# Dilated projections and all gates by seven half-size products, with the sums of h's quarters made in the memory branch

## The chip, the cores and the metric

The kernel runs on one core of one Trainium2 chip. The metric is the device time in microseconds from the first to the last instruction of one launch. The kernel before takes 2093.71 us (median of three runs, 2093.24 to 2095.69). One more execution was profiled: it took 2091.8 us, and the span of its trace is 2090.0 us. All durations below come from that execution.

## The reference

One decoder layer on 1024 tokens of width 1024, in float32. Cut to what matters here:

```python
h = rms_norm(x, g_pre_mix)
proj = h @ w_in                       # columns: MLA latents, dilated q/k/v, memory q, gates
y_mla = mla(...)                      # 8 heads, low-rank q and kv
y_dil = dilated_mixture(proj[..., OFF_KR:OFF_DIL])   # 3 groups x 4 heads x 128, q, k and v: 36 blocks of 128 columns
y_mem = mem_attention(...)            # 4 heads against 256 memory tokens
gates = sigmoid(proj[..., OFF_MEMQ:] + b_gate)       # 3 x 1024 columns: 24 blocks of 128
merged = sum(gates[n] * (y[n] @ w_br[n]) for n in 3 branches)
x = x + rms_norm(merged @ w_o)
x = x + rms_norm(conv_ffn(rms_norm(x)))              # up 1024 -> 2 x 2816, conv, silu gate, down
```

A dilated head regroups the tokens by their residue (dilation 1, 4 or 16) and attends within a band of 128 keys before each query. Its three groups are combined by their softmax denominators.

## The kernel before

Everything is kept with features on the partitions and tokens along the free axis. Each float32 operand of a product is split in two float32r parts, hi and lo (`split`: ACT writes hi at L141, DVE or POOL writes lo = x - hi at L146), and every product is three matmuls, hi*hi, lo*hi and hi*lo (`mm3`: L156, L157, L158). A projection of 128 columns over 1024 tokens is thus 8 blocks of k, times 3, times two halves of 512 tokens: 48 matmuls of 512 columns.

A second form, `winograd`, takes two blocks of 128 columns at once. It cuts the weights in four quarters (two column blocks, two halves of k) and h in four (two halves of k, two halves of the tokens), and makes the eight half-size products from seven. Sums of the weights are made on POOL (L1183, L1184, L1189, L1196), each of the seven sums is split, the products (L1179) go into four PSUM banks `f`, and DVE, ACT and POOL combine them (L1186 to L1201). A pair of blocks takes 7 x 4 x 3 = 84 matmuls of 512 columns. The right-hand sides are quarters of h and four sums of quarters, T1 to T4, which `winograd_rhs` makes (POOL and DVE at L1107 and the lines after it).

The stages, in the order of the program: startup (norm, h split into `ht`), the memory branch (to about 143 us), the latents of MLA (to about 200), MLA's eight heads (to 419.7), the dilated branch (to 926), the rest of the gates, then merge, out projection and the two FFN stages. Six of the eight tiles of h are stored to DRAM at the start (`spill_h`), because MLA uses their room for k, q and v, and loaded again at its end (`reload_h`). The dilated branch makes q, k and v of two heads at a time by plain projections, group 0's values with the tokens on the partitions (`values_by_token`, matmuls of 256 columns), and keeps them split as pages. `dil_head` then walks four pairs of 128 queries: scores, softmax (L803 to L811), transposes, the product with v, eviction (L843, L844). The first gate blocks are made by plain projections (`early_gates` and `gate_direct`), the other ten pairs by `winograd` in `all_gates`, with the outputs of the dilated and MLA branches (`dil_out`, `mla_out`) between.

Buffers are slots of named pools (`wr` raw weights, `wh` and `wl` split weights, `pg` pages, `p`, `pt`, `ht`), all of one tile pool that lives as long as the kernel. A list scheduler with a timing simulation of its own decides the order of every engine's instructions, SP's loads and stores (`load`, L161) among them. What stands in SP's queue is issued strictly in that order: an issue that waits for a buffer holds up all that stand behind it.

Of the kernel before, what the change touches and what calls it, by code (L numbers as in the profile page):

```python
# [20 lines left out]
P = 128  # L21
# [66 lines left out]
NPG, NWR, NWH, NP, NPT = 13, 4, 4, 3, 4  # L88
# [4 lines left out]
SPILLED = ((0, 0), (1, 0), (0, 1), (1, 1), (0, 2), (0, 3))  # L93


class Kern:
    def __init__(self, tc, ctx, ins, out):
        self.tc, self.nc, self.out = tc, tc.nc, out
        self.i = ins
        self.sb = ctx.enter_context(tc.tile_pool(name="sb", bufs=1))  # L100
        self.dr = ctx.enter_context(tc.tile_pool(name="dr", bufs=1, space=DRAM))
        self.n = 0
# [6 lines left out]
    def t(self, tag, bufs, shape, dt=F32):  # L109
        return self.sb.tile(shape, dt, tag=tag, bufs=bufs, name=self.name(tag))  # L110
# [10 lines left out]
    def arena(self, dt=F32R):  # L121
        return self.t("ht", 8, [P, 2, 1024], dt)
# [175 lines left out]
    def feature_unit(self, w, m0, rhs, k=KD, m=P):  # L298

        for half in range(2):  # L300
            u = self.ps("u")
            for kk in range(k):
                self.mm3(u[:m], w(kk, m0, m), [r(kk)[:, 512 * half:512 * half + 512] for r in rhs],
                         kk == 0, kk == k - 1)
            yield half, u


    def new_h(self):
        self.hA = [[self.arena() for _ in range(4)] for _ in range(2)]
        self.set_h()  # L310

    def set_h(self):
        self.hT = [lambda k, a=a: a[k // 2][:, k % 2, :] for a in self.hA]

    def startup(self):
# [39 lines left out]
        def blocks(b0):  # L355
            for q in range(4):
# [5 lines left out]
                sl = slice(b0 * P, (b0 + 2) * P)  # L362
                self.split(self.hA[0][q][:, :, sl], self.hA[1][q][:, :, sl], tp)
# [27 lines left out]
    def spill_h(self):  # L391

        self.hD = self.dr.tile([6, P, 2, S], F32, name="hD")
        for n, (hl, q) in enumerate(SPILLED):
            self.nc.gpsimd.dma_start(self.hD[n], self.hA[hl][q].bitcast(F32))

    def reload_h(self):
        for n, (hl, q) in enumerate(SPILLED):
            t = self.arena()
            for j in range(2):  # L400
                self.load(t[:, j, :].bitcast(F32), self.hD[n][:, j, :])
            self.hA[hl][q] = t
        self.set_h()
# [52 lines left out]
    def latents(self):  # L456
# [59 lines left out]
        for half in range(2):  # L516
            sl = slice(512 * half, 512 * half + 512)
            u = self.ps("u")
            for k in range(KD):
                for hl in range(2):  # L520
                    nc.tensor.matmul(u, wkr[:, k, :], self.hT[hl](k)[:, sl], start=k == hl == 0,
# [6 lines left out]
        self.cq = [lambda k, hl=hl: self.cT[hl][k] for hl in range(2)]  # L528
        self.ckv = [lambda k, hl=hl: self.cT[hl][3 + k] for hl in range(2)]
# [20 lines left out]
    def mla_start(self):  # L550
# [3 lines left out]
        self.kA, self.qA, self.vA = [[self.arena() for _ in range(2)] for _ in range(3)]  # L554
# [10 lines left out]
    def mla(self):  # L565
# [13 lines left out]
        self.w_first = self.w_cols(self.i["w_in"], OFF_DIL, page=True)  # L579
# [12 lines left out]
    def mla_v(self, hf):  # L592
# [8 lines left out]
        for b2 in range(8 // n):  # L601
            u = self.ps("u", (P, n, 256))
            for a in range(n):
                b = n * b2 + a
                for k in range(2):
                    self.mm3(u[:, a, :], [self.ckv[hl](k)[:, b * P:(b + 1) * P] for hl in range(2)],
# [91 lines left out]
    def dilated(self):  # L698
        nc, i = self.nc, self.i
# [3 lines left out]
        for hp in range(2):  # L703
            for g in range(3):
                col = lambda part: OFF_DIL + ((part * 3 + g) * DIL_HG + 2 * hp) * DH
                qk = []
                for part in range(2):
                    w = self.w_first if hp == g == part == 0 else self.w_cols(i["w_in"], col(part))
                    pair = []
                    if hp == g == part == 0:  # L710
                        first = [(half, self.ps(("u", "s")[j])) for j in range(2) for half in range(2)]
                        for kk in range(KD):
                            for x, (half, u) in enumerate(first):
                                self.mm3(u, w(kk, x // 2 * P, P), [r(kk)[:, 512 * half:512 * half + 512] for r in self.hT],
                                         kk == 0, kk == KD - 1)
                    for j in range(2):
                        d = [self.pg(dt=F32R) for _ in range(2)]
                        dil = PERM[g]
                        sc = DH ** -0.5 if part == 0 else 1.0
                        for half, u in first[2 * j:2 * j + 2] if hp == g == part == 0 else self.feature_unit(w, j * P, self.hT):  # L720
                            hs = slice(512 * half, 512 * half + 512)
                            if g == 0:
                                self.split(d[0][:, hs], d[1][:, hs], u, sc)
                                continue
                            n = 512 // dil
                            uv = u.rearrange("p (l r) -> p l r", r=dil)
                            ls = slice(half * n, (half + 1) * n)
                            if part == 0:
                                dv = [self.perm(t, g)[:, ls, :] for t in d]
                                self.split(dv[0], dv[1], uv, sc)  # L730
                                continue
# [702 lines left out]
```

## Time and profile before

| | |
|---|---|
| time, median of three runs | 2093.71 us |
| profiled execution, its span | 2091.8 us, 2090.0 us |
| PE busy | 1970.1 us, 94% |
| DVE, ACT, POOL busy | 1375.8 (66%), 927.0 (44%), 637.4 us (30%) |
| mean granted TensorE clock | 0.985 |
| dilated branch | 419.7 to about 926 us |
| gates, merge | to about 1160, to 1293 us |
| DMA traffic | 217.81 MB, mean 104 GB/s |

Times in the rows are microseconds from the start of the span. Matmuls are pipelined: a group's mean (394 ns for 512 columns) is a latency, and what one costs the engine is the distance from its start to the next one's. L followed by a number is a line of the kernel. SPq is SP's sequencer, which issues DMAs. The granted clock (PEclk) is a share of the higher of TensorE's two levels.

### The profile page before, as it was taken

What the parts mean: (1) busy time and instruction counts of PE and PEld (TensorE: products, weight loads), DVE (VectorE), ACT (ScalarE), POOL (GpSimd) and SP (SyncE); (2) the same over time, 40 slices, a digit from 0 to 9 for tenths busy, and PEclk for the clock granted to TensorE, in tenths of its full rate; (3) what the DMA queues carried; (4) which work ended last, traced back from release to release, by engine and by line L of the source; (5) the groups of instructions that cost most, each with busy time, mean ns of one, the idle gap of its engine ahead of it and who ended that gap; (6) DMA issues with size and microseconds to landing.
All of it is one profiled execution on the core that took longest, in us unless ns stands there. A gap on an engine that the chain in (4) does not pass through costs nothing.

```text
span 2090.0 us, 25550 instructions
## 1 busy us (share of the span) xinstructions
PE 1970.1 (94%) x9550; PEld 1639.2 (78%) x9550; DVE 1375.8 (66%) x1944; ACT 927.0 (44%) x1737; POOL 637.4 (30%) x417
## 2 busy tenths in 40 slices
PE   6999889799999999998899999998999999989994
PEld 6887677689888988876787888887888888768863
DVE  7645777725354354478655566658777777699999
ACT  6544565624354244444334332334454445455433
POOL 3100111100010000025454040004555555487766
PEclk9999999999999999999999999999999999999997
DMA  8411101341322221212665762231222222433322
GB/s 278 163 64 36 26 22 41 116 132 43 89 72 60 82 82 46 57 47 87 201 216 198 267 225 102 101 91 60 91 73 88 83 91 71 149 133 101 121 81 81
DMA packets 150858, 217.81 MB, mean 104 GB/s; under 512 B 22737, under 2 KB 114558, under 8 KB 149966
## 3 DMA queue, kind: packets, MB, share of 16 engines
q1 hardware_dynamic: 137422, 192.93, 28.8%
q0 software_dynamic: 13312, 23.25, 3.2%
q8 instruction: 75, 1.23, 0.2%
q14 instruction: 49, 0.40, 0.1%
HBM read 159.13 MB, written 55.85 MB: 103 GB/s over the span
## 4 chain that ended last, share of the span: by engine, by line
PE 59%; issue 17%; DVE 14%; DMA 4%; ACT 3%; POOL 2%; SPq 0%; DVEq 0%; POOLq 0%; ACTq 0%
PE f L1179 20%; PE u L156 7%; PE u L157 6%; PE u L158 6%; PE f L156 4%; PE f L157 4%; PE f L158 4%; PE f L1258 3%; DVE wl L146 3%; DVE wh L146 3%; DVE pt L146 2%; DVE ht L1263 2%; PE o L827 1%; POOL oD L689 1%; DMA wr<-dD 1%
## 5 line engine op out<-in xcount | busy, mean ns | idle before, releaser
L156 PE MATMUL u<-ht,wh 128*128 128x512 f32 x672 | 264.4, 394 | 0.9 <-ACT p L467 0.4
L157 PE MATMUL u<-ht,wh 128*128 128x512 f32 x672 | 264.2, 393 | 0.0
L158 PE MATMUL u<-ht,wl 128*128 128x512 f32 x672 | 263.3, 392 | 0.0
L141 ACT ACTIVATE wh<-wr 128x512 fp32r<-128x512 f32 (+3 forms) x164 | 127.3, 798 | 152.9 <-PE u L157 47.2
L1179 PE MATMUL f<-ht,wh 128*128 128x512 f32 x636 | 159.3, 394 | 8.9 <-ACT wh L141 5.7
L1179 PE MATMUL f<-ht,wl 128*128 128x512 f32 x636 | 156.9, 391 | 0.4 <-DVE p L1192 0.4
L1179 PEld LDWEIGHTS f<-ht,wh 128*128 128x128 f32 x636 | 120.6, 190 | 35.8 <-ACT wh L141 6.4
L156 PEld LDWEIGHTS u<-ht,wh 128*128 128x128 f32 x672 | 126.3, 188 | 26.0 <-ACT ht L141 0.9
L158 PEld LDWEIGHTS u<-ht,wl 128*128 128x128 f32 x672 | 126.4, 188 | 25.0
L157 PEld LDWEIGHTS u<-ht,wh 128*128 128x128 f32 x672 | 126.4, 188 | 23.7
L1179 PEld LDWEIGHTS f<-ht,wl 128*128 128x128 f32 x636 | 120.1, 189 | 26.1 <-issue 0.8
L146 DVE TENSOR_TENSOR wl<-wr,wh 128x1024 fp32r<-128x1024 f32 (+2 forms) x74 | 90.9, 1231 | 69.4 <-ACT wh L141 69.2
L846 POOL DMA_DIRECT2D dD<-y x24 | 13.2, 550 | 394.4 <-DVE y L844 394.4
L1179 PE MATMUL f<-pg,wh 128*128 128x512 f32 x444 | 121.0, 394 | 8.7 <-ACT pg L141 5.4
L1179 PE MATMUL f<-pg,wl 128*128 128x512 f32 x448 | 122.4, 393 | 2.9 <-DVE p L1193 1.7
L141 ACT ACTIVATE pg<-u 128x512 fp32r<-128x512 f32 (+2 forms) x90 | 61.2, 680 | 135.1 <-PE u L158 121.4
L1179 PEld LDWEIGHTS f<-pg,wh 128*128 128x128 f32 x444 | 84.3, 190 | 27.7 <-ACT pg L141 6.1
L146 DVE TENSOR_TENSOR pt<-t,pt 128x512 fp32r<-128x512 f32 (+2 forms) x148 | 88.6, 608 | 25.4 <-ACT pt L141 24.4
L1179 PEld LDWEIGHTS f<-pg,wl 128*128 128x128 f32 x448 | 84.6, 189 | 21.3 <-DVE p L1193 2.2
L146 DVE TENSOR_TENSOR pg<-u,pg 128x256 fp32r<-128x256 f32 (+2 forms) x60 | 37.1, 618 | 96.7 <-ACT pg L141 96.5
L141 ACT ACTIVATE pt<-t 128x512 fp32r<-128x512 f32 (+2 forms) x148 | 76.7, 537 | 39.4 <-PE t L671 21.1
L1258 PE MATMUL f<-wh,pt 128*128 128x512 f32 x312 | 80.9, 397 | 13.2 <-DVE wh L146 6.8
(379 smaller groups left out, 5102.4 us busy)
## 6 DMA issues: line engine op xcount, KB each, us to landing
wr<-in_w_in_dram SPq DMA_DIRECT2D x67, 512.0 KB
wr<-in_w_ffn_up_dram SPq DMA_DIRECT2D x88, 256.0 KB
p<-gD SPq DMA_DIRECT2D x24, 512.0 KB
gD<-p SPq DMA_DIRECT2D x22, 512.0 KB
actD<-p SPq DMA_DIRECT2D x22, 512.0 KB
pg<-actD SPq DMA_DIRECT2D x22, 512.0 KB
hD<-ht POOLq DMA_DIRECT2D x6, 1024.0 KB, 7.2
ht<-hD SPq DMA_DIRECT2D x12, 512.0 KB
```

The source lines that it names most:

```text
L141: self.nc.scalar.activation(out, src, AF.Copy, scale=float(scale))
L146: (eng or self.nc.vector).tensor_tensor(out, src, h, op=OP.subtract)
L156: mm(out, l[0], r[0], start=start, stop=False)
L157: mm(out, l[0], r[1], start=False, stop=False)
L158: mm(out, l[1], r[0], start=False, stop=stop)
L689: nc.gpsimd.dma_start(self.oD[:, 64 * h:64 * h + 64, 256 * m:256 * m + 256], y.rearrange("p a q -> p (a q)"))
L827: mm = lambda out, l, r, st: nc.tensor.matmul(out, l, r, start=st, stop=False, skip_group_check=True)
L846: nc.gpsimd.dma_start(self.dD[g, h][:, 512 * (pr // 2):512 * (pr // 2) + 512], y)
L1179: nc.tensor.matmul(out, l[a], r[c], start=start and k == n == 0, stop=k == 3 and n == 2, skip_group_check=True)
L1258: nc.tensor.matmul(u[t], l[j][:, x, t * P:(t + 1) * P], r[j][:, y], start=j == m == 0, stop=j == n - 1 and m == 2, skip_group_check=True)
L1263: vt(acc[d][:, t], acc[d][:, t], u[t], op=OP.add)
```

## The change

All 36 projections of the dilated branch are made by `winograd`, 18 pairs of blocks in the order in which the heads need them, and so are the first two pairs of gate blocks: `early_gates` and `gate_direct` go. q, k and v are kept unsplit, in five pages `rp`, and `dil_head` splits what a pair of queries needs; values always come by transposes. h is stored as quarter tiles (`hQ`, 4 blocks of k by 512 tokens). T1 to T4 are made by the new `spill_T` behind the memory branch and stored to DRAM as 8 tiles of 1 MB (as sixteen stores of 512 KB); only four tiles of h are stored. `reload_h` loads these twelve tiles, 12 MB in place of 6. The pools are opened and closed by stage (`room`), the dilated branch has four `f` banks and one `s` bank in place of two `u` and two `s`, and its first weights are no longer loaded into pages during MLA (`w_first` goes). `mla_out` moves from the dilated branch into the gates.

```diff
     def spill_h(self):
-        self.hD = self.dr.tile([6, P, 2, S], F32, name="hD")
-        for n, (hl, q) in enumerate(SPILLED):
-            self.nc.gpsimd.dma_start(self.hD[n], self.hA[hl][q].bitcast(F32))
+        self.hD = self.dr.tile([4, P, 4, 512], F32, name="hD")
+        for x in range(2):
+            for hl in range(2):
+                self.nc.gpsimd.dma_start(self.hD[2 * x + hl], self.hQ[x, 0][hl].bitcast(F32))
+    def spill_T(self):
+        self.tTD = self.dr.tile([8, P, 4, 512], F32, name="tTD")
+        B = {q: [[t[:, 2 * j:2 * j + 2, :] for j in range(2)] for t in self.hQ[q]] for q in self.hQ}
+        T = self.winograd_rhs(B, lambda n: [[self.pg((P, 2, 512), F32R) for _ in range(2)] for _ in range(2)], True, True)
     def reload_h(self):
+        T = {}
+        for n in (1, 3, 2, 4):
+            T[n] = [self.arena(shape=(P, 4, 512), tag="hT") for _ in range(2)]
+            for hl in range(2):
+                self.load(T[n][hl].bitcast(F32), self.tTD[2 * (n - 1) + hl])
+        for x in range(2):
+            self.hQ[x, 0] = [self.arena(shape=(P, 4, 512)) for _ in range(2)]
...
-        self.w_first = self.w_cols(self.i["w_in"], OFF_DIL, page=True)
...
     def dilated(self):
+        heads = [(g, 2 * hp + j) for hp in range(2) for g in range(3) for j in range(2)]
+        todo = [(part, g, h) for g, h in heads for part in range(3)]
+        done, n = [], 0
+        for i, (g, h) in enumerate(heads):
+            while len(done) < 3 * i + 3:
+                two = todo[len(done):len(done) + 2]
+                cols = [OFF_DIL + ((part * 3 + g1) * DIL_HG + h1) * DH for part, g1, h1 in two]
+                pages = [self.t("rp", NRP, [P, 1024]) for _ in two]
+                self.winograd(self.in_weights(cols), self.B, self.t("S", 1, [P, 2, 4, P]),
+                              self.t("tt", 1, [P, 2, 512]), *pages, [PERM[g1] for _, g1, _ in two])
+                done += pages
+            self.dil_head(g, h, *done[3 * i:3 * i + 3])
...
+            qp = self.t("qs", 2, [P, 2, 256], F32R)
+            self.split(qp[:, 0], qp[:, 1], q[:, 256 * pr:256 * pr + 256], DH ** -0.5)
...
+            self.split(kp[:, 0, :n], kp[:, 1, :n], k[:, k0:k0 + n], eng=nc.gpsimd)
...
     def all_gates(self):
-        self.gate_direct(2, 2, False)
-        turns = [(2, 4), (2, 6)] + [(n, c) for n in range(2) for c in range(0, 8, 2)]
+        turns = [(n, c) for n in (2, 0, 1) for c in range(0, 8, 2)]
...
+            if p % 2 == 0 and 0 < p <= 8:
+                self.mla_out(p // 2 - 1)
...
     def run(self):
+        with self.room("ht"):
+            with self.room("pg", "wh", "wl"), self.room("hx", "p", "pt", "wr"):
...
+                    self.mem_branch()
+                    self.spill_T()
+                    self.latents()
...
+            with self.room("hT"):
+                with self.room("wr", "wv", "S", "tt", "rp", "p2", "e", "ks", "qs", "vs"), \
+                        self.phase(f=4, s=1, t=2, o=1) as self.psum:
+                    self.reload_h()
+                    self.dilated()
+                with self.room("wr", "wv", "S", "tt", "gp", "o4"), self.phase(f=8) as self.psum:
+                    self.all_gates()
```

The scheduler places the instructions anew. Three places on SP follow, each as it stands before and after. The first is the loads of the latents' weights (`wr` from `in_w_in_dram`), at the end of the memory branch. Before:

```order
L161 DMA pg_626<-in_positions_dram 128x1x128
L161 DMA wr_1444<-in_w_in_dram 128x4x256
L161 DMA wr_1450<-in_w_in_dram 128x4x256
L161 DMA wr_1570<-in_w_in_dram 128x8x128
L161 DMA wr_1691<-in_w_in_dram 128x4x256
L291 DMA tD<-pg_625 8x16x128 x2
L161 DMA wr_1697<-in_w_in_dram 128x4x256
```

After:

```order
L1043 DMA tTD<-pg_1451 128x1024
L1043 DMA tTD<-pg_1453 128x1024
L1043 DMA tTD<-pg_1455 128x1024
L1043 DMA tTD<-pg_1459 128x1024
L1043 DMA tTD<-pg_1457 128x1024
L161 DMA wr_1522<-in_w_in_dram 128x4x256
L1043 DMA tTD<-pg_1461 128x1024
L161 DMA wr_1528<-in_w_in_dram 128x4x256
```

Five stores of T (`tTD`, from the pages that the split writes) now stand ahead of the first weights, and more between the rest.

The second is the end of MLA, on SP: the reload of h (`hD` into `ht`), and the first weights of the dilated branch. Before, with the first weights in pages (`pg_4018`, `pg_4024`):

```order
L161 DMA wr_2638<-in_w_ukv_dram 128x2x512
L161 DMA ht_4035<-hD 128x1024 x2
L161 DMA pg_4018<-in_w_in_dram 128x4x256
L161 DMA pg_4024<-in_w_in_dram 128x4x256
L161 DMA ht_4038<-hD 128x1024 x2
L161 DMA ht_4041<-hD 128x1024 x2
L161 DMA ht_4044<-hD 128x1024 x2
L161 DMA ht_4047<-hD 128x1024 x2
L161 DMA wr_4170<-in_w_in_dram 128x4x256
L161 DMA wr_4176<-in_w_in_dram 128x4x256
L161 DMA wr_4294<-in_w_in_dram 128x4x256
```

After, from the second tile of h on (`hT` are the tiles of T1 to T4):

```order
L161 DMA ht_4126<-hD 128x1024 x2
L161 DMA ht_4131<-hD 128x1024 x2
L161 DMA hT_4109<-tTD 128x2048
L161 DMA hT_4110<-tTD 128x2048
L161 DMA hT_4113<-tTD 128x2048
L161 DMA hT_4114<-tTD 128x2048
L161 DMA hT_4117<-tTD 128x2048
L161 DMA hT_4118<-tTD 128x2048
L161 DMA hT_4121<-tTD 128x2048
L161 DMA hT_4122<-tTD 128x2048
L161 DMA ht_4132<-hD 128x1024 x2
L161 DMA wr_4144<-in_w_in_dram 128x4x128 x2
```

The first weights of the dilated branch (`wr_4144`) moved behind eight tiles of T and the last two loads of h.

The third is the end of the gates, on SP: stores of gates (`gD` from the pages of the gates), and the first loads of merge (`yD`, and the weights `in_w_br_mem_dram`). Before:

```order
L161 DMA wr_9762<-yD 128x1024
L985 DMA gD<-p_9352 128x1024
L161 DMA wr_9768<-yD 128x1024
L161 DMA wr_9774<-yD 128x1024
L161 DMA wr_9780<-yD 128x1024
L985 DMA gD<-p_9502 128x1024
L985 DMA gD<-p_9503 128x1024
L161 DMA wr_9786<-in_w_br_mem_dram 128x4x256
L161 DMA wr_9854<-in_w_br_mem_dram 128x4x256
L161 DMA wr_9922<-in_w_br_mem_dram 128x4x256
```

After:

```order
L912 DMA gD<-gp_9952 128x1024
L912 DMA gD<-gp_9953 128x1024
L912 DMA gD<-gp_10087 128x1024
L912 DMA gD<-gp_10088 128x1024
L161 DMA wr_10224<-yD 128x1024
L161 DMA wr_10230<-yD 128x1024
L161 DMA wr_10236<-yD 128x1024
L161 DMA wr_10242<-yD 128x1024
L161 DMA p_10254<-gD 128x1024
L161 DMA p_10285<-gD 128x1024
L161 DMA p_10322<-gD 128x1024
L161 DMA wr_10248<-in_w_br_mem_dram 128x4x256
```

Before, merge's first loads stand among the stores of gates; now they stand behind the last of them, and the first weights behind four tiles of `yD` and three of `gD`.

## Rows read from the trace of the kernel before

**Rows 1.** Windows by stage: busy us (instructions) per engine, PEclk, DMA share, GB/s.
```profile
70.00:143.00 73.00, 73.00 (x435) 64.35 (x435) 40.06 (x89) 37.96 (x97) 4.84 (x9) 1.00 0.27 95
143.00:201.00 58.00, 57.64 (x280) 47.45 (x279) 24.42 (x48) 23.46 (x42) 1.49 (x2) 1.00 0.10 32
...
505.00:589.00 84.00, 84.00 (x429) 71.23 (x427) 36.07 (x57) 35.85 (x70) 5.52 (x6) 1.00 0.23 70
...
841.00:926.00 85.00, 80.14 (x404) 67.71 (x403) 49.71 (x84) 36.42 (x86) 11.71 (x10) 0.98 0.15 43
926.00:960.00 34.00, 30.06 (x123) 24.05 (x122) 17.97 (x24) 11.24 (x19) 7.90 (x4) 0.90 0.17 56
960.00:1000.00 40.00, 36.99 (x155) 29.43 (x154) 35.39 (x32) 17.34 (x25) 22.25 (x12) 0.97 0.43 132
1000.00:1171.00 171.00, 163.56 (x712) 133.96 (x712) 104.23 (x108) 73.40 (x105) 76.24 (x48) 0.99 0.65 214
...
1470.00:1825.00 355.00, 354.66 (x1565) 293.45 (x1563) 254.92 (x278) 167.28 (x241) 192.81 (x110) 1.00 0.28 89
```

**Rows 2.** PE timeline, group 0's values: start us, us, engine, line, operands.
```profile
462.34 0.28 PE L156 MATMUL u<-wh,ht 128*128 128x256 f32 x1
...
465.70 0.28 PE L157 MATMUL u<-wl,ht 128*128 128x256 f32 x1
```

**Rows 3.** PE timeline, transposes of values.
```profile
642.07 1.03 PE L773 MATMUL t<-cst,p 128*128 128x128 f32 x8
```

**Rows 4.** PE timeline, last gate product and first merge products.
```profile
1157.74 0.39 PE L156 MATMUL f<-pg,wh 128*128 128x512 f32 x1
...
1160.92 2.88 PE L1179 MATMUL f<-pg,wh 128*128 128x512 f32 x12
```

**Rows 5.** Windows of 5 us around the reload of h; columns as above.
```profile
410.00:415.00 5.00, 3.04 (x17) 2.04 (x17) 3.70 (x7) 3.60 (x8) 1.15 (x2) 1.00 0.72 212
415.00:420.00 5.00, 4.61 (x23) 3.48 (x24) 1.91 (x4) 1.31 (x3) 0.08 (x1) 1.00 1.01 312
420.00:425.00 5.00, 5.00 (x24) 4.13 (x23) 0.59 (x2) 1.21 (x2) 0.80 (x1) 1.00 1.10 342
425.00:430.00 5.00, 5.00 (x24) 4.14 (x23) 2.28 (x2) 1.90 (x2) 0.00 (x0) 1.00 1.02 344
```

**Rows 6.** Waits of SP, 360 to 460 us: total, times, longest us.
```profile
SPq L161 <- PE s L158: 36.5, 2, 24.4
```

**Rows 7.** The page, part 6: a store of 1 MB, last number us to landing.
```profile
hD<-ht POOLq DMA_DIRECT2D x6, 1024.0 KB, 7.2
```

**Rows 8.** Groups of instructions, ACT: count, busy us, mean ns, idle before.
```profile
L141 ACT ACTIVATE wh<-wr 128x512 fp32r<-128x512 f32 x89 | 52.1, 622 | 55.7 <-DMA wr<-in_w_in_dram 22.3 <-DVE wh L146 11.4 <-POOL wr L1189 9.2
...
L811 ACT ACTIVATE p<-p,st 128x256 f32<-128x256 f32 x64 | 31.7, 497 | 14.5 <-DVE st L809 14.5
...
L984 ACT ACTIVATE p<-p,par 128x1024 f32<-128x1024 f32 x20 | 22.9, 1144 | 4.5 <-DVE p L1200 2.7 <-issue 0.9 <-DVE p L1198 0.7
```

**Rows 9.** Groups of instructions, DVE.
```profile
L146 DVE TENSOR_TENSOR wl<-wr,wl 128x512 fp32r<-128x512 f32 x88 | 81.1, 925 | 10.2 <-ACT wl L141 10.2
...
L146 DVE TENSOR_TENSOR pt<-t,pt 128x512 fp32r<-128x512 f32 x80 | 54.1, 685 | 20.0 <-ACT pt L141 19.1
...
L146 DVE TENSOR_TENSOR wh<-pg,wh 128x512 fp32r<-128x512 f32 x42 | 53.5, 1275 | 31.3 <-ACT wh L141 31.1
...
L1192 DVE TENSOR_TENSOR p<-p,f 128x512 f32<-128x512 f32 x29 | 19.9, 686 | 31.9 <-PE f L1179 29.7 <-ACT p L1186 2.2
...
L844 DVE TENSOR_TENSOR y<-y,o 128x256 f32<-128x256 f32 x48 | 19.8, 415 | 20.1 <-ACT y L843 19.7
```

**Rows 10.** Groups of instructions, POOL.
```profile
L1196 POOL TENSOR_TENSOR wr<-wr,pg 128x512 f32<-128x512 f32 x19 | 42.1, 2214 | 76.6 <-DVE wl L146 39.7 <-DVE wh L146 32.3 <-issue 4.6
...
L1183 POOL TENSOR_TENSOR pg<-wr,wr 128x512 f32<-128x512 f32 x19 | 25.2, 1324 | 5.0 <-DMA wr<-in_w_ffn_up_dram 5.0
...
L1107 POOL TENSOR_TENSOR p<-ht,ht 128x1024 f32<-128x1024 f32 x4 | 10.4, 2606 | 19.0 <-DVE pt L146 19.0
```

More of the change, by code (lines that the diff above doesn't have):

```diff
@@ L1 @@
 import math
-from contextlib import ExitStack
+from contextlib import ExitStack, contextmanager
 import numpy as np
@@ L109, in t @@
     def t(self, tag, bufs, shape, dt=F32):
-        return self.sb.tile(shape, dt, tag=tag, bufs=bufs, name=self.name(tag))
+        return self.where.get(tag, self.sb).tile(shape, dt, tag=tag, bufs=bufs, name=self.name(tag))
     def pg(self, shape=(P, 1024), dt=F32):
@@ L778, in dil_head, with in_weights @@
+    def in_weights(self, cols):
+        raw = []
+        for kh in range(2):
+            r = self.t("wr", self.n_wr, [P, 4, 2, P])
+            for j, c in enumerate(cols):
+                self.load(r[:, :, j, :], self.i["w_in"][kh * 512:(kh + 1) * 512, c:c + P].rearrange("(k p) c -> p k c", p=P))
+            raw.append(r)
+        return raw
+    def dil_head(self, g, h, q, k, v):
         nc = self.nc
@@ L822, in dil_head @@
                 nc.tensor.transpose(tp[:, n, :], p[:, a, kt * P:(kt + 1) * P], self.ident)
-            e = self.pt((P, nb, 2, P))
+            e = self.t("e", 2, [P, nb, 2, P], F32R)
             self.split(e[:, :, 0, :], e[:, :, 1, :], tp[:, :nb, :])
-            vt = lambda kt: [v[hl][kt // 4][:, kt % 4, vc:vc + P] for hl in range(2)]
+            before = vp if pr > 0 else None
+            vp = self.t("vs", 2, [P, 2, 2, P], F32R)
+            tv = self.ps("t", (P, 2, P))
+            for a in range(2):
+                nc.tensor.transpose(tv[:, a, :], v[:, tl[a] * P:(tl[a] + 1) * P], self.ident)
+            self.split(vp[:, 0], vp[:, 1], tv)
+            vt = lambda kt: [(vp if kt >= tl[0] else before)[:, hl, kt % 2, :] for hl in range(2)]
             o = self.ps("o", (P, 2, 2, P))
@@ L1110, in parts @@
                 self.split(T[n][0][j], T[n][1][j], t)
+                if spill:
+                    for hl in range(2):
+                        nc.sync.dma_start(self.tTD[2 * (n - 1) + hl][:, 2 * j:2 * j + 2, :], T[n][hl][j].bitcast(F32))
             a, b = [self.t("wr", NWR, [P, 2, 512]) for _ in range(2)]
@@ L1172, in winograd, with seen, to @@
         u2, p5 = tt[:, 0, :], tt[:, 1, :]
+        def seen(t, r):
+            return t if r == 1 else t.rearrange("p (l r) -> p l r", r=r)
+        def to(gv, half):
+            t, r = (ug, uv)[gv], order[gv]
+            n = 512 // r
+            return t[:, 512 * half:512 * half + 512] if r == 1 else \
+                t.rearrange("p (r l) -> p l r", r=r)[:, half * n:half * n + n, :]
+        og, ov = order
         def product(out, src, b, start=True):
@@ L1210, in tiles @@
         def tiles(n):
-            t = [self.t("ht", 8, [P, 4, 512], F32R) for _ in range(2)]
+            t = [self.arena(shape=(P, 4, 512)) for _ in range(2)]
             return [[t[hl][:, 2 * j:2 * j + 2] for j in range(2)] for hl in range(2)]
```

247 lines of the change are left out of this document (72 added, 175 removed).

## The prediction

> **What bounds the kernel now.** I read the windows by stage first, then PE's timeline for what one matmul costs, then the SP queue and the DMA rates at the stage borders. The windows show PE busy in 73.00 of 73 us of the memory branch, 57.64 of 58 of the latents, and 84.00 of 84 in the middle of the dilated branch, with DVE at 36 us of these 84 [rows 1]. The kernel is PE time, laid end to end, and the borders between its stages are closed. The only open places near the change are 841 to 1000 us, where PE misses 4.9 + 3.9 + 3.0 = 11.8 us, and the gates, 7.4 us in 171 [rows 1]. So two questions decide: how many matmuls go, and whether the borders stay closed.
>
> **What PE saves.** The FFN's long stretch gives 354.66 us for 1565 matmuls, 0.2266 us for 512 columns [rows 1]. 28 steps from 462.34 to 465.70 give 0.120 us for 256 columns [rows 2]. Eight transposes span 1.03 us with a latency of 0.27, so 0.109 us each [rows 3]. Before, the 36 dilated blocks are 1536 matmuls of 512 columns and 384 of 256: 348.1 + 46.1 = 394.2 us. After, 18 pairs x 84 = 1512: 342.6 us. The two gate pairs fall from 192 to 168, 5.4 us less. Values of group 0 need 32 more transposes, 3.5 us. Saving: 51.6 + 5.4 - 3.5 = 53.5 us.
>
> The stretch that this concerns runs from 419.7 to the end of the last gate product. That product ends at 1160.92 + 12 x 0.2266 = 1163.6, and 14 matmuls of merge (3.2 us, from 1157.74) already stand ahead of it [rows 4], so an equivalent border is 1160.5: 740.8 us. Its matmuls, counted (2600 of 512, 808 of 256, 236 transposes), are 712 us; 28.8 us are idle or at the lower clock. After, the same count is 658.5 us. What has to be added to 658.5 is the forecast.
>
> **Border 1, end of MLA (30 us).** Before, the first product of the dilated branch follows MLA's last without a gap, since its weights were in pages and h had mostly come. After, the order shows one queue on SP: the third tile of h, eight tiles of T, the last tile of h, then the first weights. The third tile of h takes a buffer that MLA's last scores read; a load in that position waited 24.4 us for a score product before [rows 6], to about 410 us. From there 10 tiles of 1.05 MB and 0.26 MB of weights must pass, 10.75 MB. Until 420 the rows give 212 and 312 GB/s, 2.6 MB; then 342 and 344 GB/s [rows 5], so 8.1 MB take 23.7 us, to 443.7. A store of 1 MB landed 7.2 us after its issue [rows 7]; at 343 GB/s it takes 3.1, so a start-up of 0 to 4 us, of which I take 2. Then a split of 0.62 us [rows 8]: the first product starts at about 446.5, 27 us after MLA's end. The second product needs sums of weights on POOL, 1.3 us each [rows 10], and its weights come behind the first: 3 us more. Bounds: 23 if all 10.75 MB pass at 344 from 410, 36 if at the mean of 262 that 410 to 420 shows. Nothing covers it: in this stage's order no product of another stage stands on PE.
>
> On DMA speed, the row shows 344 GB/s at most, while loads are queued. The Trainium skill's "DMA: Bandwidth & Descriptors" (Bandwidth) measures about 425 GB/s for 16 MB alone; by it this border would be 4.5 us and border 4 2.3 us shorter, and the time 2110. The row decides, since it is this kernel's own load of h.
>
> **Inside the dilated branch (6 us).** Per pair of blocks: 7 splits, ACT 0.62 each and DVE 0.69 to 0.93, four evictions on DVE at 0.69, and on POOL five sums of 1.3 to 2.2 us [rows 8 to 10]. Per pair of queries: about 2.8 us of DVE and 3.1 of ACT, from the softmax's, split's and eviction's rows [rows 8, 9]. For 18 pairs and 48 query pairs: DVE 269 to 290, ACT 250 to 280, POOL 140 to 180 us, beside some 427 us of PE: up to 68%, 66%, 42%. The FFN shows the same products at DVE 72% and POOL 54% with PE at 354.66 of 355 [rows 1], so 0 is the lower bound; the gates lose 7.4 us in about nine such pairs [rows 1], 0.8 each, 15 for 18, and with one score bank I set the upper bound at 20. I take 6, nearer the FFN, because head work fills PE between pairs.
>
> **Border 2, dilated to gates (14 us).** The last head stands alone on PE at the end. Its four query pairs cost ACT about 3.1 us each, 14 with the run-out, against 5.8 us of matmuls: about 9 idle. SP issues the gates' first weights only after it has stored the last head's statistics, which wait for the last exponentials; the load and split end about 2 us after the last product. Then the second product again waits for POOL, 3 us. Before, the first gates stood here beside the heads. Bounds 6 to 20.
>
> **Gates (10 us).** Twelve pairs, at the loss that 926 to 1171 shows: 3.9 + 3.0 + 7.4 = 14.3, less what the sums of T took there, now gone: 10, bounds 6 to 14.
>
> **Border 3, gates to merge (18.5 us).** Before, merge's products are woven into the last gate pair [rows 4]. After, all loads of merge stand behind the last store of a gate. The store waits for the last sigmoid, 1.14 us [rows 8] plus eviction and sum, 2.4 together. Then seven tiles (four yD, three gD) and the first weights, 4.2 MB at 343 GB/s: 12.2; start-up 2 and a split of 1024, at twice the 0.62, 1.2; the issue of the weights waits for a slot that the first yD frees, 0.7. Bounds: 10 if the weights overtake, 22.
>
> **Border 4, memory branch to latents (22 us).** Before, latents' products stand among the last heads, hence 73.00 of 73. After, the first sums of T hold the `wr` buffers, and five stores of T stand ahead of latents' first weights. So the last head runs alone: 8.7 us of matmuls along a chain of softmax and splits of about 17 us, 8 idle. Then T's chain, with an add of 2.6 us on POOL [rows 10], a difference and a split on DVE and ACT beside it, the stores' issue, and the weights' transfer: about 14 us more. Nothing else is ready for PE. Bounds 8 to 30; the low end is a chain that runs wholly beside the memory branch, where DVE has 33 of 73 us free [rows 1].
>
> **Clock.** In 926 to 960 the granted clock was 0.90 [rows 1], which is 3.4 us lost at the lower level, beside idle places. Four long idle stretches come in; I add 5, bounds 0 to 10.
>
> **The sum.** From the profiled execution: 2091.8 - 740.8 + 658.5 + (30 + 6 + 14 + 10 + 18.5) + 22 + 5 = 2115.0. The median of the runs lies 1.9 above that execution: 2117. The saving would have to meet added idle of less than 82 us in all to be seen; I count 105. With the terms' errors combined the forecast's own range is 2099 to 2135.
>
> **Rivals.**
> - *The weights pass the queued tiles (faster, 2079).* At borders 1 and 3 the transfers queued on SP share the engines, so that the first weights land within about 5 us of their issue instead of behind 10.5 and 3.7 MB. Then border 1 falls to 5 and border 3 to 6 us: 2117 - 25 - 12.5 = 2079.5. It decides if the first dilated product starts before about 428 us. For it: no row shows in which order loads that are queued together land. Against it: 342 and 344 GB/s in two successive windows [rows 5] say that the engines were full, and in before's queue the last of the reload was the last to be issued. The Trainium skill ("DMA: Bandwidth & Descriptors", Queues, rings and completion order) has descriptors consumed in ring order, which speaks against it too.
> - *T is early (no change, 2092).* If T's chain ends inside the memory branch and the weights come in time, border 4 falls to 5, and if SP is free border 2 falls to 6: 2117 - 17 - 8 = 2092. For it: DVE's free 33 us. Against it: POOL's adds of 2.6 us and the order of the stores.
> - *DVE and POOL block each other (slower, 2147).* The lo part of a split took 0.685 us from PSUM, 0.925 from `wr`, 1.275 from the pages that POOL writes at the same time [rows 9]. If all 126 splits of the dilated branch go at 1.275 and the 0.35 us is on the path, it costs up to 44; at two thirds of that, 30. Against it: the FFN's 354.66 of 355. The Trainium skill's "SBUF — State Buffer" (Who interferes with whom) names an exclusive lock between a DVE operation with two SBUF inputs and a GpSimd operation; the rows agree in direction.
>
> **How the numbers follow.** Forecast 0.62; weights passing 0.13; T early 0.10; DVE and POOL 0.15. A change of under 0.2%, about 4 us, cannot be told from none. Faster: 0.13 and a third of T early, with a little of the forecast's low tail, 0.17. Same: 0.06. Slower: 0.77. The range leaves out about a tenth at either end: 2080 to 2148.
>
> **What would show it.** In the profile after: PE idle of about 27 us behind MLA's last product, released by the first weights' DMA or its split; idle of about 20 before the latents and before merge; 84 of 84 in the middle of the dilated branch, which is then about 430 us long. The forecast is wrong if the first dilated product follows MLA within 10 us, if PE is full across 143 us, or if windows inside the dilated branch show PE under 90%.

## The result, and the profile after

The changed kernel takes 2118.97 us, median of four runs (2118.27 to 2119.55), against 2094.03 us (2093.24 to 2095.69, four runs) before: a ratio of 1.0118, 95% interval 1.0100 to 1.0135. It is slower by 1.2%, and 2 us above the forecast. Its span is 2117.8 us, 27.8 longer, at a mean granted clock of 0.965 (0.985 before).

The stages as windows (columns of [rows 1]):

```profile
70.00:141.00 71.00, 68.03 (x403) 58.39 (x403) 40.85 (x96) 36.39 (x95) 6.12 (x8) 0.97 0.12 43
141.00:154.00 13.00, 1.09 (x5) 0.80 (x5) 10.71 (x8) 5.66 (x6) 4.30 (x4) 0.50 0.73 255
154.00:175.00 21.00, 21.00 (x85) 17.00 (x85) 15.49 (x11) 9.30 (x13) 4.43 (x2) 0.91 1.05 355
...
442.00:464.00 22.00, 0.27 (x2) 0.00 (x0) 0.42 (x1) 0.63 (x2) 0.80 (x1) 0.56 1.03 378
464.00:480.00 16.00, 15.58 (x59) 12.37 (x60) 6.85 (x10) 5.63 (x10) 7.49 (x6) 0.86 0.41 107
...
505.00:589.00 84.00, 84.00 (x438) 71.53 (x437) 59.76 (x95) 48.34 (x121) 35.74 (x32) 1.00 0.21 57
841.00:903.00 62.00, 57.38 (x297) 47.74 (x296) 43.74 (x88) 34.13 (x99) 18.71 (x20) 0.99 0.12 32
903.00:908.00 5.00, 0.54 (x3) 0.24 (x2) 0.42 (x1) 0.43 (x2) 0.54 (x1) 0.50 0.44 114
908.00:960.00 52.00, 50.41 (x212) 40.42 (x213) 35.17 (x43) 21.94 (x38) 30.24 (x19) 0.96 0.69 200
960.00:1000.00 40.00, 32.20 (x124) 25.80 (x123) 26.14 (x22) 10.74 (x17) 23.36 (x16) 0.84 0.68 234
1000.00:1060.00 60.00, 54.47 (x232) 43.96 (x231) 39.39 (x35) 21.11 (x31) 30.43 (x20) 0.96 0.73 235
1060.00:1166.00 106.00, 106.00 (x476) 87.72 (x476) 48.23 (x64) 43.65 (x64) 42.89 (x31) 1.00 0.32 106
1166.00:1185.00 19.00, 0.69 (x4) 0.23 (x2) 5.59 (x5) 6.43 (x6) 0.00 (x0) 0.65 0.92 328
1185.00:1200.00 15.00, 14.95 (x58) 12.23 (x59) 12.44 (x13) 8.48 (x8) 0.00 (x0) 0.88 0.88 284
```

Four stretches in which PE stands: 141 to 154, 442 to 464, 903 to 908 and 1166 to 1185, and a fifth, spread, in the gates at 960 to 1060. Before, the first was 73.00 of 73 and the second did not exist. In each of the four the granted clock is 0.50 to 0.65 in the mean, so wholly or for the most part at the lower level, and it is still 0.91 in the 21 us behind the first and 0.88 in the 15 us behind the last. Between 505 and 841 four windows of 84 us are full, one of them shown.

What PE waited for, whole span (engine and line, releaser: total us, times, longest):

```profile
PE f L1124 <- ACT wv L141: 27.2, 2, 22.1
PE f L156 <- ACT wh L141: 18.4, 1, 18.4
PE u L156 <- ACT wh L141: 11.9, 1, 11.9
```

These three lines hold the borders MLA to dilated (the wait of 22.1), gates to merge, and memory branch to latents, in this order of size; the other 5.1 of the first line are the border from the dilated branch to the gates. Each ends with ACT's split of the first weights, that is, with a load. The queue in front of the second border, on SP (start, us, what it issues):

```profile
410.12 21.90 SPq L161 DMA_DIRECT2D ht<-hD  x4
432.08 11.22 SPq L161 DMA_DIRECT2D hT<-tTD  x8
443.40 1.24 SPq L161 DMA_DIRECT2D ht<-hD  x2
447.18 16.40 SPq L161 DMA_DIRECT2D wr<-in_w_in_dram  x6
```

The first weights are issued behind eight tiles of T, as the order had shown, and ACT's split of them waits for their load:

```profile
463.74 0.63 ACT L141 ACTIVATE wv<-wr 128x512 fp32r<-128x512 f32 x1 [18.52 <-DMA wr<-in_w_in_dram]
```

The rates there, which answer to [rows 5]:

```profile
435.00:440.00 5.00, 3.66 (x17) 2.84 (x16) 2.91 (x6) 2.88 (x6) 0.80 (x1) 0.72 1.04 410
440.00:445.00 5.00, 2.06 (x10) 1.11 (x8) 1.18 (x2) 1.04 (x3) 0.00 (x0) 0.96 1.03 381
445.00:450.00 5.00, 0.00 (x0) 0.00 (x0) 0.42 (x1) 0.21 (x1) 0.80 (x1) 0.50 1.01 417
450.00:455.00 5.00, 0.00 (x0) 0.00 (x0) 0.00 (x0) 0.00 (x0) 0.00 (x0) 0.50 1.02 388
455.00:460.00 5.00, 0.00 (x0) 0.00 (x0) 0.00 (x0) 0.00 (x0) 0.00 (x0) 0.50 1.01 405
```

Mean 400 GB/s, where [rows 5] gave 343. In the gates, what DVE stood for from 905 to 1166:

```profile
DVE o L868 <- DMA o<-dD: 10.9, 3, 3.9
...
DVE o L872 <- DMA o<-dD: 7.8, 4, 3.2
```

L868 and L872 are the multiplications of `dil_out`. Behind them in DVE's queue stand splits and evictions of the gate pairs.

From the distances between PE's starts the difference can be closed. MLA's last product starts at 442.00 instead of 418.15 (+23.9). From there to merge's first product it takes 743.0 us (742.3 before, up to the equivalent border at 1160.5; +0.7). From merge's first product to the end it takes 932.7 (929.5, +3.2: merge begins at the lower clock, its first 200 products take 47.2 us where 0.2266 each would be 45.3; the other 1.3 us are spread behind them and not explained). Together 27.8, the whole difference of the spans. The 419.7 at which the prediction lets the dilated branch begin lies behind that branch's first six products, which start at 418.26; with 419.7 the first two parts are +22.6 and +2.0.

### The profile page after: what moved, and what is told of

Same layout as the page of the kernel before. It is cut to its first block, busy times and chain, and to the rows that moved or that the text cites. A ratio compares the mean times of both kernels' runs of the same rounds, so it can differ in the third digit from the quotient of the medians.

```text
span 2117.8 us, 25694 instructions
## 1 busy us (share of the span) xinstructions
PE 1938.3 (92%) x9150; PEld 1600.4 (76%) x9150; DVE 1481.0 (70%) x2115; ACT 979.5 (46%) x1931; POOL 829.2 (39%) x563
## 4 chain that ended last, share of the span: by engine, by line
PE 61%; DVE 14%; issue 14%; DMA 6%; POOL 2%; ACT 2%; SPq 0%; DVEq 0%; POOLq 0%; ACTq 0%
PE f L1124 41%; PE f L156 3%; PE f L157 3%; PE f L158 3%; PE f L1203 3%; DVE wl L146 2%; DVE pt L146 2%; DVE ht L1208 2%; DVE wh L146 2%; DMA o<-dD 1%; PE o L800 1%; DMA wr<-in_w_in_dram 1%; POOL oD L702 1%; DVE wv L146 1%; PE t L789 1%
## 5 line engine op out<-in xcount | busy, mean ns | idle before, releaser
L1124 PE MATMUL f<-hT,wv 128*128 128x512 f32 x1440 | 356.0, 396 | 9.6 <-DVE gp L1138 7.2
L1124 PEld LDWEIGHTS f<-hT,wv 128*128 128x128 f32 x1440 | 269.0, 190 | 66.0 <-issue 7.6
L1124 PE MATMUL f<-ht,wv 128*128 128x512 f32 x1080 | 270.2, 399 | 31.9 <-ACT wv L141 27.2
L1124 PEld LDWEIGHTS f<-ht,wv 128*128 128x128 f32 x1080 | 204.4, 192 | 75.2 <-ACT wv L141 27.8
L146 DVE TENSOR_TENSOR wv<-wr,wv 128x512 fp32r<-128x512 f32 x150 | 145.7, 975 | 117.9 <-ACT wv L141 115.3
L141 ACT ACTIVATE wv<-wr 128x512 fp32r<-128x512 f32 x150 | 93.8, 631 | 135.5 <-PE f L1124 51.2
L141 ACT ACTIVATE wh<-wr 128x512 fp32r<-128x512 f32 (+2 forms) x101 | 71.9, 743 | 59.2 <-PE f L157 28.7
L1203 PE MATMUL f<-pt,wl 128*128 128x512 f32 x312 | 82.0, 401 | 13.4 <-DVE pt L146 6.7
L1134 POOL TENSOR_TENSOR wr<-wr 128x512 f32<-128x512 f32 x49 | 81.5, 1663 | 0.0
L1203 PE MATMUL f<-wl,wh 128*128 128x512 f32 x300 | 77.4, 397 | 4.1 <-DVE wl L146 4.1
L1037 POOL TENSOR_TENSOR wr<-pg,pt 128x1024 f32<-128x1024 f32 x4 | 12.7, 3164 | 164.4 <-DVE p L1008 142.2
```

What stands on the lines that cost most here:

```text
L141: self.nc.scalar.activation(out, src, AF.Copy, scale=float(scale))
L146: (eng or self.nc.vector).tensor_tensor(out, src, h, op=OP.subtract)
L1124: nc.tensor.matmul(out, l[a], r[c], start=start and k == n == 0, stop=k == 3 and n == 2, skip_group_check=True)
L1134: pt(A[1, 0], A[0, 0], A[1, 0], op=OP.subtract)
L1203: nc.tensor.matmul(u[t], l[j][:, x, t * P:(t + 1) * P], r[j][:, y], start=j == m == 0, stop=j == n - 1 and m == 2, skip_group_check=True)
```

## The experiments

Times are single runs unless an interval is given; the runs of before on the same chips gave 2091.5 to 2096.9 us, so the times of two single runs that lie within some 5 us of each other do not tell them apart; the gaps do. A gap is the distance between two starts on PE. Each edit is of the changed kernel.

### The memory branch: what T costs there

```diff
-        T = self.winograd_rhs(B, lambda n: [[self.pg((P, 2, 512), F32R) for _ in range(2)] for _ in range(2)], True, True)
+        for n in range(4):
+            for hl in range(2):
+                self.nc.gpsimd.dma_start(self.tTD[2 * n + hl], self.hQ[n // 2, n % 2][hl].bitcast(F32))
```

> This kernel leaves out the sums T1 to T4: four quarters of h are stored in their place by POOL's queue, so the reload moves the same bytes. Theory (the memory branch's border is the price of T's sums and stores): the idle 12 us before the latents and the loss in the last head go, MLA's last product moves from 442.0 back to 420 to 423 us, and the time falls by 19 to 22 us to about 2097; all later borders stay as they are. Rival (the split of the pools by stage makes that border): MLA ends at 440 or later and the time stays within 4 us of 2119.

Measured: 2100.16 us. MLA's last product starts at 417.69 (442.00 in the changed kernel), and the stretch is closed again:

```profile
141.00:154.00 13.00, 13.00 (x64) 11.00 (x63) 2.75 (x5) 4.58 (x9) 0.54 (x1) 1.00 0.15 50
```

The other borders stay (22.95 us at MLA's end, 17.9 before merge). So T costs 24 us at its place, 19 in the end; 4 of the 5 us between come back in the gates, which take 261.8 us here and 257.7 in the changed kernel, for a reason that was not looked for.

What of T costs it? First the stores, moved off SP (`nc.sync.dma_start(self.tTD...` to `nc.gpsimd.dma_start`):

> Only the queue of T's sixteen stores changes, from SP to POOL. Theory A (latents' weights wait because they stand behind the stores on SP): MLA ends 10 to 14 us earlier, about 2106. Theory B (the weights wait for the wr buffers, which T's sums hold until 147 to 149 us in the trace after, so that the queue alone is not the cause): MLA's end moves by less than 4 us and the time is 2115 to 2121. I hold B.

Measured: 2122.47 us, and the gap grows from 12.3 to 15.4; MLA's last product starts 4.8 us later, a little more than theory B allowed. The stores on SP are not the cause. Then the latents' first weights loaded ahead of T:

```diff
+                    self.w_lat = self.w_cols(self.i["w_in"], 0)
                     self.spill_T()
...
-        w = self.w_cols(i["w_in"], 0)
+        w = self.w_lat
```

> T is made and stored as before, on the same queue; only the load and split of the latents' first weights stand ahead of it in the program. Theory (the border is the wait for these weights, not T's load on DVE and POOL): products of the latents fill the last heads again, the idle before the latents falls from 12 to under 4 us, MLA ends at 423 to 428, and the time is about 2101 to 2105. Rival (T's 40 us of DVE and 16 of POOL are what costs there): MLA still ends after 436.

Measured: 2117.58 us. The idle time moves into the latents, which then wait on ACT (one gap of 17.6 us from 149.7):

```profile
141.00:154.00 13.00, 9.12 (x46) 7.39 (x45) 12.96 (x10) 5.20 (x6) 5.60 (x4) 0.94 0.59 208
143.00:201.00 58.00, 40.79 (x182) 33.57 (x181) 30.66 (x34) 20.16 (x29) 9.66 (x4) 0.82 0.61 204
```

My theory that the late weights are the price fell: MLA's last product still starts at 439.78. DVE is full in 141 to 154 (12.96 of 13), and ACT evicts the latents' first unit only at 166.21, behind the last split of T that it makes ahead of it, from 165.25. So T's work itself stands in front of the latents'. Then T in two pieces, each of half the blocks of k, inside the memory branch:

```diff
-        for j in range(2):
+        for j in js:
...
+                if (c, j) in ((0, 1), (1, 0)):
+                    self.spill_T(((0, 1), (1, 0)).index((c, j)))
```

> T's sums are made in two halves inside the memory branch (one behind its second head, one behind its third), in place of one block behind its last head; same work, same queue. What the last runs left: the load order alone gave 2 us back, leaving T out gave 24. Theory (T's chain through POOL, DVE and ACT, each in order, holds up the evictions of whatever PE does beside it; it costs because it comes in one piece at a place where PE has little queued): MLA ends between 422 and 432, time 2099 to 2109. Rival (T's work costs its 20 us wherever it stands, since DVE and ACT are what the memory branch and the latents lack): MLA ends after 436, time over 2113.

Measured: 2121.57 us, gaps of 6.2 and 10.3 inside the memory branch, MLA's last product at 443.84. The price came along: the theory fell and its rival held.

### MLA to dilated: bytes ahead of the first weights

```diff
         for n in (1, 3, 2, 4):
+            if n != 1:
+                T[n] = T[1]
+                continue
```

> This kernel leaves out the loads of T2, T3 and T4 (6.3 MB of the 12.6 MB of the reload); T1 is read in their place. Theory (the first dilated product waits until all bytes queued ahead of its weights have passed, at the 395 GB/s that the trace after shows): its start moves from 464.2 to about 448 to 450, the idle behind MLA from 22 to 6 to 8 us, the time to about 2103. Rival (the weights pass the queued tiles, or the wait is for the pools' room): the gap stays over 18 us.

Measured: 2106.68 us, gap 8.6 in place of 22.4. The first dilated product starts at 448.85 instead of 464.42, 15.6 us earlier with six tiles of 1.05 MB fewer in the queue. Most of the wait is the queue's bytes. The quotient of the two, 404 GB/s, is not a rate, since here SP stands before the last tile of h:

```profile
430.95 0.90 SPq L161 DMA_DIRECT2D hT<-tTD  x2
440.59 0.80 SPq L161 DMA_DIRECT2D ht<-hD  x2
441.48 21.55 SPq L161 DMA_DIRECT2D wr<-in_w_in_dram  x10
```

That tile waits 8.7 us for MLA's last products to give back its buffer, and what is left of the gap begins there. Then nothing left out, only the order:

```diff
+                    self.raw0 = self.in_weights([OFF_DIL + part * 3 * DIL_HG * DH for part in range(2)])
                     self.reload_h()
...
-        for n in (1, 3, 2, 4):
-            T[n] = [self.arena(shape=(P, 4, 512), tag="hT") for _ in range(2)]
-            for hl in range(2):
-                self.load(T[n][hl].bitcast(F32), self.tTD[2 * (n - 1) + hl])
+        sums(1, 3, 2)
         for x in range(2):
...
+        sums(4)
```

`sums` holds the four lines taken out, the loop over x loads the tiles of h, and the first pair of blocks takes its weights from `raw0`.

> The first dilated weights are asked for ahead of the reload, in buffers that MLA frees early, and the tiles of the reload come in the order of their use (T4 last); the same bytes move. Theory (the gap behind MLA is the queue of bytes ahead of the weights): the first product starts within 8 us of MLA's last, later ones wait a little for their tiles, 10 to 18 us are saved, time about 2101 to 2109. Rival (bytes are the limit whatever their order, as no product can run far without its T): less than 5 us are saved, over 2114.

Measured: 2103.81 us, gap 7.0. In 442 to 464, where PE had 0.27 us, it now has 15.66 with the transfers still at 368 GB/s:

```profile
442.00:464.00 22.00, 15.66 (x56) 12.28 (x57) 6.34 (x10) 5.42 (x10) 6.32 (x5) 0.77 1.03 368
```

### Gates to merge: one set of buffers

In the order of the changed kernel no instruction of merge stands ahead of the last of the gates on any engine, since merge's buffers open on memory that the gates' buffers must first give back.

```diff
-                with self.room("wr", "wv", "S", "tt", "gp", "o4"), self.phase(f=8) as self.psum:
+                ends.enter_context(self.room("wr", "wh", "wl", "p", "pt", side="right"))
+                self.psum = ends.enter_context(self.phase(f=8))
...
-        with self.room("ht", "pg", "wh", "wl", "p", "pt", "wr"), self.phase(f=8) as self.psum:
+        with ends, self.room("ht", "pg"):
             self.merge()
```

and merge's first weights are loaded ahead of its first `yD`.

> The gates and merge share one set of pools (raw and split weights, pages) and one PSUM pool, at the other end of the memory, so that merge's loads may be placed among the gates' stores, with its first weights ahead of yD; the gates use the same numbers of buffers but four instead of five for the branch outputs. Theory (the border is the closing of the gates' pools: nothing of merge is placed before the last use of their tiles): the gap at the gates' end falls from 18.7 to 3 to 8 us, time about 2105 to 2109. Rival (the gap is the transfer itself, whatever the pools): it stays over 14 us.

Measured: 2095.95 us, no gap at all (18.7 before the edit, first merge product 0.6 us behind the last gate product):

```profile
1166.00:1185.00 19.00, 18.99 (x84) 15.73 (x85) 14.92 (x16) 9.61 (x10) 0.00 (x0) 1.00 0.93 324
```

The transfers are as dense as in the changed kernel (324 and 328 GB/s), but gates' products now stand beside them. Of the 23.7 us by which the span is shorter, 18.1 are the gap, 3.1 shorter gates and 3.0 lie behind merge's first product, where merge now starts at the full clock (1.0 us of it in its first 200 products; the rest is not explained). Half a microsecond was lost ahead of the gates. The run changed the buffers and the order of merge's loads at once; how much the order alone would give was not tried.

### The gates: what the 26 us are

The gates take 257.7 us for 12 pairs x 84 x 0.2266 + 32 transposes x 0.109 = 231.9. First, `dil_out` one turn later (`p % 2 == 1 and p >= 3`, head `p // 2 - 1`):

> dil_out of each head comes one gate turn pair later. Theory (the 26 us that the gates take over their matmuls come from DVE standing at dil_out's multiplications, which wait for tiles asked for too late, while splits and evictions queue behind it): the stall moves or shrinks, the gates take 245 to 252 us instead of 257.9, time 2107 to 2114. Rival (the number of DVE and POOL operations in those turns is what stalls): the gates stay within 3 us of 257.9.

Measured: 2129.01 us, 10 slower; the gates take 267.6 us. The stall moved and grew, and the theory's 245 to 252 did not come. Then the sums of `dil_out` taken away:

```diff
-        for g in range(3):
-            a = self.t("o4", 5, [P, 1024])
-            self.load(a, bass.AP(tensor=self.aD.tensor, offset=self.aD[g, h].offset, ap=[[0, P], [1, S]]))
-            o = self.t("o4", 5, [P, 1024])
-            self.load(o, self.dD[g, h])
...
-                nc.vector.tensor_tensor(av, self.perm(o, g), av, op=OP.mult)
-                nc.gpsimd.tensor_tensor(tot, tot, a, op=OP.add)
+        tot = self.t("o4", 5, [P, 1024])
+        self.load(tot, self.dD[0, h])
```

> The changed kernel with dil_out's sums left out: per head one load of dD and one store in place of six loads, three multiplications and two adds. The gates take 257.7 us in the changed kernel for 231.9 us of matmuls, 26 lost, where 10 had been forecast. Theory (DVE stands in order at dil_out's multiplications until their loads land, and the splits and evictions behind it hold up PE, with the lower clock after each such gap): without them the gates lose 10 us or less, in all 16 us or more less than the changed kernel, about 2102. Rival (the gates lose by their own chain, sums on POOL, splits and evictions, and by mla_out): they still lose 20 or more, 2113 or above.

Measured: 2095.97 us, 23 less. The gates run from 908.8 to 1144.6, 235.8 us, 4 lost. From 960 to 1060, where PE had stood 13.3 us and, counted by its matmuls, had lost 21.7, nothing is lost:

```profile
960.00:1000.00 40.00, 40.00 (x182) 33.09 (x182) 18.99 (x25) 16.25 (x24) 19.35 (x16) 1.00 0.53 171
1000.00:1060.00 60.00, 60.00 (x274) 49.67 (x273) 27.90 (x38) 24.51 (x37) 27.47 (x20) 1.00 0.41 133
```

So 22 of the 26 us are `dil_out`. Whether by its loads or its multiplications this run does not part, since it took both.

### Together

Both border edits at once:

> Both border edits at once: the dilated branch's first weights ahead of the reload of h with T4 loaded last, and one set of buffers and one PSUM phase for gates and merge. Apart they gave 15 and 23 us. Theory (each border is its own wait, nothing is shared): they add up, 2119 - 15 - 23 = 2081, with a gap of about 7 us at MLA's end and none ahead of merge, and the kernel is then faster than both. Rival (a gain at one border is given back later, since DVE and the queues are shared): the gates lose more and the time is about 2095, as with the second edit alone.

Measured: 2087.23 us (2082.82 to 2087.59, five runs), 0.9958 of before, interval 0.9945 to 0.9972. Faster than both kernels, 6 us above the sum. The gap at MLA's end is 5.6 us and merge has none. In its profiled execution (span 2085.7, the longest of the five) the dilated branch starts 14.4 us earlier than in the changed kernel, at 450.04, and the gates 12.7. From the gates' first product to the end it takes 1189.7 us, 4.8 more than with the second edit alone. That is where most of the 6 us are, but not in the gates, as the rival had it (255.1 us, 254.5 with the second edit alone): 4.3 lie behind merge's first product. Their cause stays open; the five runs are 4.8 us apart, and the shortest lies 2 above the sum.

To this kernel, `dil_out` in twelve steps, one behind each pair of gate blocks:

```diff
-            if p % 2 == 1 and p // 2 < 4:
-                self.dil_out(p // 2)
+            self.dil_out(p // 3, p % 3)
```

> The kernel with both border edits, and dil_out cut in its twelve steps (one group of one head, two loads and one multiplication), one behind each pair of gate blocks, where it was three steps behind every second of the first eight pairs. Theory (in the gates DVE stands in order at multiplications whose loads come in bursts of six tiles through four or five slots, and the evictions behind it hold up PE): with two loads a pair the gaps in the gates shrink from about 15 us to under 6, some 10 us faster than with both border edits alone. Rival (the wait is for any load at all, since the slots free late): twelve short waits in place of four long ones, the same time within 3 us.

Measured: 2089.54 us, the same within those runs' spread. DVE's waits for `dD` stay (27.5 us, and 27.4 with both border edits alone). The rival held: spreading the steps does not shorten the wait for the loads.

And T in four small pieces:

```diff
+                        if 1 <= 2 * h + pr // 2 <= 4:
+                            self.spill_T(2 * h + pr // 2 - 1)
```

where each call makes the four sums of one block of k, all on POOL, in pages instead of `wr` buffers, splits them and stores them.

> The kernel with both border edits, and the sums of h's quarters made in four pieces of one k-block of 512 tokens, behind the second half of head 0, both halves of head 1 and the first half of head 2 of the memory branch, all sums on POOL, the splits as before on ACT and DVE, no wr buffer taken. Theory (T costs by the DVE and ACT time and the buffers that it takes in one block; in small pieces, with the sums on the engine that is idle there, the memory branch has room): the gap ahead of the latents shrinks from 12 to under 5 us, MLA's end from 441 to about 427, some 14 us faster than with both border edits alone. Rival (any T work there stands in the heads' chains on DVE and ACT, as the two-piece run showed): gaps inside the memory branch take its place, within 4 us of the same time or slower.

Measured: 2068.48 us, one run, 19 less than with both border edits and 25.8 less than before on that chip. MLA's last product starts at 425.89 (444.46 with both border edits alone, 418.15 before the change). The memory branch and the border behind it:

```profile
70.00:143.00 73.00, 68.86 (x388) 58.74 (x387) 59.52 (x94) 41.49 (x99) 44.56 (x35) 0.98 0.46 160
128.00:141.00 13.00, 13.00 (x79) 11.45 (x79) 11.14 (x21) 8.07 (x22) 3.80 (x4) 1.00 0.59 206
141.00:154.00 13.00, 13.00 (x78) 11.41 (x78) 5.20 (x12) 6.42 (x17) 0.88 (x2) 1.00 0.11 42
```

POOL carries 44.56 us where it had 4.84 [rows 1], PE loses 4 us in the branch and none at the border. T still costs some 8 us by MLA's end. The two-piece run stood in the heads too and gained nothing, so the place alone is not it. Which of the three differences (small pieces, sums on POOL, no `wr` buffers) does most was not tried apart.

## Why the prediction was right, step by step

- **The sign and the size.** Forecast +23 us (2117 against 2093.71), measured +24.9 between the medians and +27.8 between the spans. From the end of MLA's last product to merge's first, 742.8 us, 84.3 stand above the count of 658.5: 22.2 + 12.1 + 5.5 + 25.8 + 18.7, forecast at 78.5, and 5 more for the clock. The 12.1 and 25.8 are stage times less counted matmuls, so they close by construction. What supports the count, and with it the saving of 53.5 us, is the run without `dil_out` (gates of 235.8 us for a count of 231.9) and the full windows.
- **Border 4** (22): +23.9 at MLA's end, 22.6 from the prediction's 419.7. The split into a last head alone and the late weights was not shown. With the weights early the price stayed; with T left out it went, and with T in four pieces on POOL most of it (MLA's last product at 425.89). It is T's own work where it stands as one block.
- **Border 1** (30): 22.2. The mechanism was right (the queued bytes, shown by the runs with fewer tiles and with another order), the rate was mis-sized. The row of 343 GB/s was an observed rate, not the limit; here 400 came. The Trainium skill's "DMA: Bandwidth & Descriptors" (Bandwidth) was nearer with its 425 than my row: by it I had made the border 25.5. (The 2.3 us that the prediction takes off border 4 in that place belong to border 3.) The second product's 3 us for POOL did not show either: its first sums ran beside the first product, which is long at the lower clock.
- **Inside the dilated branch and border 2** (6 and 14): 12.1 and 5.5. From 505 to 841 PE never stands, with DVE at 71%, so DVE and POOL do not block each other here at a price. Counted by its matmuls (54.1 us from 841 to 903), some 8 of the 12.1 us are the last head's, 4.6 of them idle, which I had counted to the border; 2.2 lie at the branch's start, at a granted clock of 0.86 from 464 to 480, and 2 are spread over the rest. So border 2 is 13.6 for 14 and the inside 4 for 6, but the 6 were meant for waits on DVE and POOL inside the branch, and those were not there.
- **Gates** (10): 25.8. This is the term that was mis-sized, and by the way it was read. I took the idle time of before's last stretch, 14.3 us, for its whole loss and subtracted T's sums. The idle time did not fall, and it is not the whole loss. In the windows below, before (first) and after, PE stands 14.4 and 14.9 us. The matmuls of the first (939, of them 936 of 512 columns) count 212.4 us, so some 22 were lost there already, 8 of them not as idle time; after, it is 25.8, of them 11 not idle. The mean granted clocks of 0.97 and 0.96 over these lengths make 7 and 10 us of that, an estimate. For this part the prediction had only the 5 us for the clock.

```profile
926.00:1160.00 234.00, 219.61 (x939) 178.32 (x938) 150.76 (x156) 94.93 (x142) 105.56 (x64) 0.97 0.53 172
908.00:1166.00 258.00, 243.09 (x1041) 197.89 (x1042) 148.93 (x164) 97.44 (x150) 126.92 (x84) 0.96 0.55 175
```

  The cause was in the trace of before too: `dil_out` alone costs 22 after the change, as the run without it shows, and before, DVE stood 19.8 us for the same loads (L895 and L899 are its multiplications there):

```profile
DVE wr L899 <- DMA wr<-dD: 11.3, 5, 5.0
DVE wr L895 <- DMA wr<-dD: 8.5, 3, 3.3
```

  So the gates lose only some 4 us more than before. What `mla_out`, now in the same stretch, and the loss of merge's products beside the last gates add to that was not tried.
- **Border 3** (18.5): 18.7, for the reason given, all loads behind the last gate. Behind it 3.2 us more are lost, of them 1.9 at merge's start at the lower clock: part of the 5 for the clock.
- **The rivals.** Weights pass the queued tiles: no, they are issued at 447.18 and split at 463.74, and the first dilated product starts at 464.42. T is early: not in this kernel, but the four-piece run comes near that case. DVE and POOL block each other: no.

That the total is nearly exact is luck: border 1 was 8 us too large and the gates 16 too small, and most of what the 5 for the clock stood for is inside the measured pieces. Neither of the two errors is as large as the 25 us measured, so the sign did not hang on them.

## What to carry to other kernels

A saving on the bounding engine is worth what the stage borders leave of it: before counting matmuls, ask for each border which load the first product needs and what is queued ahead of it. Buffers opened by stage make such borders; one set across two stages (with the next stage's first weights asked for early) and the first weights ahead of bulk loads gave back 23 and 15 us here without changing a product. Work moved to a stage with idle engines is not free: here it cost 24 us in one block and as much in two pieces, and 8 in four pieces on the idle engine without the buffers that the next stage's loads need. And idle time is not the whole loss of a stretch: its matmuls, counted at their full rate, against its length show what the idle time leaves out, 22 us for 14 in the gates before the change.

## What the runs showed of the hardware that was not expected

- The reload ran at 381 to 417 GB/s in five windows of 5 us, before at 342 and 344 [rows 5]. The loads of T have rows of 8 KB (128x2048), those of h before 4 KB (128x1024); that this is the reason was not tested. In the 21 us from 154 the rate was 355, on a mix of stores and loads.
- A border costs more than its gap. Behind the 18.7 us ahead of merge the granted clock was 0.88 for 15 us, and merge's first 200 products took 47.2 us; with the gap closed they took 46.2.
